# A hybrid encoder step: the forget-gate chain in five parts, a square sum three pairs on, memory values moved, and half of w_xo split there

## The chip, the cores and the metric

The kernel runs on one core of a Trainium2 chip. The metric is the device time of one execution in microseconds (us). Engines are named PE (TensorE, matmul), ACT (ScalarE), DVE (VectorE), POOL (GpSimd) and SP (SyncE, which issues most of the loads).

## The reference: what is computed

One layer on 512 prompt frames and 32 sample frames (544 columns in all), width 2048, in f32:

```python
gb, gc, hin, q, k, v = splits of rmsnorm(x) @ w_in           # 6 x 1024 outputs, 8 more for the gate
logf = log_sigmoid(z[..., o6:] + b_f)                        # 8 heads x 544 frames
yc = gb * short_conv(gc * hin)                               # 3 taps
ya = fox_attention(q, k_all, v_all, cumsum(logf))            # softmax with a forget bias
x += concat(rmsnorm(yc, g_conv_out), rmsnorm(ya, g_attn_out)) @ w_out
mk, mv = splits of rmsnorm(mem) @ w_xkv                      # 256 memory tokens, 4 heads
x += softmax(q_x mk) mv @ w_xo
x += square(relu(rmsnorm(x) @ w_up)) @ w_down
y = rmsnorm(x, g_final)
```

`logf`, the keys and values, the last conv rows and the memory keys and values are outputs too.

## The kernel before

Columns are the 544 frames, handled as two halves of 272. Each f32 product is made from three matmuls: operands are split into a high part (`hi`, fp32r, an ACT copy) and a low part (`lo`, a DVE subtraction), and hi·hi, hi·lo and lo·hi are summed in PSUM. `split` (L84, L85) makes both; for weights the tiles are called `whi` and `wlo`, four buffers each, one per 512 columns. A weight tile is loaded by SP into one of three `raw` buffers (128x1024, 512 KB), `weights` (L93) and `raw_block` (L220).

Where two output blocks share inputs, `seven` (L240) replaces eight block products by seven (Strassen's scheme): seven products of 24 matmuls each, called here X(b11), Y(t1), X(t2), Y(b22), X(t3), Z(b21), X(t4). The weights of t2 and b22 are sums `s2` and `s4` that DVE makes (L230); X and Y are copied out between products by ACT as `p15` and `u23` (`p` and `u` in the profile; L259, L263), so the next product into X or Y waits for that copy. The 22 pairs of the input projection (0 to 21, about 21 us each, from about 72 us) and the MLP's up projection run so. The trace order of each engine is what the scheduler of the tile framework made of the program's order; each engine works its instructions strictly in that order.

The gate: `emit_logf` makes the 8 extra outputs before the pairs; `chain_logf` (L357), called behind pair 0, turns them into `logf` and its running sums: z, e, Exp, w, Ln, a correction with a RECIPROCAL, two scans (`cum`, `cs`), the negated `neg` and `ncs` for later DMAs. `turn_logf`, behind pair 1, transposes `cum`. The readers are the attention heads, after pair 21.

The conv group: `on_gb` squares each gated block into `acc_c`; behind pair 9, the last conv pair, `rb_c = rstd(acc_c)` makes 1/rms by a square-sum matmul (`ssq`, L176), Ln and Exp on ACT and four DVE operations per half. Its reader is the output projection after pair 21.

Cross-attention (from 823 us): memory keys (L785, `w_xk`), memory values (L799, `w_xv`, eight raw tiles of 12 matmuls of 512 columns), four queries `xq` (`w_xq`, eight raw tiles), and per head scores, softmax, transposes and values, placed between the queries by hand. Then `w_xo`: 16 output blocks of 24 matmuls, eight raw tiles, two blocks each. Behind each block `xo_done` adds it to x (`x2r`, L938), squares it into `acc_3` and, for every second block, makes the operands of the MLP's `seven` (`operands`, L199). `rb_3 = rstd(acc_3)` comes behind the last block and before the first `seven` unit of the MLP.

Of the kernel before, what the change touches and what calls it, by code (L numbers as in the profile page):

```python
# [41 lines left out]
def hybrid_step(  # L42
# [156 lines left out]
    def operands(x, b11, ts, tags):  # L199
        hi, lo = two(b11)[:, 0], two(b11)[:, 1]  # L200
        split(hi, lo, x[:, 0])
        t = ts.rearrange("p (a b c) -> p a b c", a=2, b=2)
        x4 = x.rearrange("p (a b) c -> p a b c", a=2)
        dve.tensor_tensor(t[:, :, 0], x4[:, :, 1], x4[:, 0], ALU.subtract)
        for a in range(2):
            dve.tensor_tensor(t[:, a, 1], x[:, 3 - a], t[:, 0, a], ALU.subtract)
        o = {"b11": (hi, lo)}
        o["b21"], o["b22"] = both(x[:, 2:], tags[1])
        o["t1"], o["t2"] = both(t[:, 0], tags[0])
        o["t3"], o["t4"] = both(t[:, 1], tags[2])  # L210
        return o
# [6 lines left out]
    def raw_block(src, pl, tag):  # L218
        raw = pl.tile([128, 1024], F32, tag=tag, name=tag, bufs=3 if tag == "raw" else 4)
        sp.dma_start(raw, src)  # L220
        return raw
# [18 lines left out]
    def seven(pl, ops, ws, out, scale, mid, prefetch):  # L240
# [25 lines left out]
        product(X, w, "t2", False)  # L266
        act.activation(u23[:, 0], X, AF.Copy)
# [89 lines left out]
    def chain_logf(z16):  # L357
        z, lf, e, w = tmp("z"), tmp("lf"), tmp("e"), tmp("w")
        z, lf, e, w = z[:8, :T], lf[:8, :T], e[:8, :T], w[:8, :T]
# [114 lines left out]
    for i, pair in enumerate(pairs):  # L474
# [315 lines left out]
    ps = mm_tile()  # L790
    for p in range(8):
        hi, lo = weights(w_xv[p])
        for kk in range(2):
            k = 2 * p + kk
            c = slice(512 * kk, 512 * kk + 512)
            for t in range(2):
                d = slice(128 * t, 128 * t + 128)
                for n, (x, w) in enumerate(((mem[k][0], hi), (mem[k][0], lo), (mem[k][1], hi))):
                    pe.matmul(ps[:, t], x[:, d], w[:, c], start=k == 0 and n == 0, stop=k == KD - 1 and n == 2)  # L799
    for t in range(2):  # L800
        mf = tmp("mv")[:, :512]
        dve.tensor_scalar(mf, ps[:, t], rcol[:, t:t + 1], None, ALU.mult)
        pool.dma_start(o_mv[128 * t:128 * t + 128], mf)
        split(mvs[t][0], mvs[t][1], mf)
# [28 lines left out]
    def x_scores(h, q):  # L833
        P = xp.tile([128, 4, NMEM], F32, tag="P", name="xP")
# [19 lines left out]
    def x_transpose(h, P):  # L854
        PT = []
        for kt in range(2):
# [3 lines left out]
            hi = xp.tile([128, SEQ], F32R, tag=f"pth{kt}", name="xpth")  # L860
            lo = xp.tile([128, SEQ], F32R, tag=f"ptl{kt}", name="xptl")
# [4 lines left out]
    def x_values(h, PT):  # L866
# [35 lines left out]
    for h in range(HX):  # L902
        qs[h] = evac_xq(h, xq(h))
        if h == HX - 1:
            Pss = xs_scores()
            sa(h)
            sb(h - 1)
            sc(h - 1)
        else:
            sa(h)  # L910
            if h < HX - 2:
                sb(h)
                sc(h)
# [22 lines left out]
    def xo_done(m, ps):  # L936
# [5 lines left out]
        if i == 0:  # L942
            xgs[j] = up.tile([128, 4, TH], F32, tag="form", name="x")
# [43 lines left out]
    def plain(m, h):  # L987
        f = up.tile([128, 2, 2, TH], F32R, tag="form", name="form")
# [5 lines left out]
    def forms(i, h1, h2):  # L994
# [9 lines left out]
        for x, (j, k) in ((t12, (1, 2)), (b, (5, 3)), (t34, (4, 6))):  # L1004
            f = up.tile([128, 2, 2, TH], F32R, tag="form", name="form")
# [25 lines left out]
    up_cm.__exit__(None, None, None)  # L1031

# [241 lines left out]
```

## Time and profile before

| | us |
|---|---|
| three runs | 2391.26, 2392.85, 2392.91 |
| median | 2392.85 |
| profiled execution | 2392.07 |
| its span | 2390.3 |
| PE busy in the span | 2325.7 |
| DVE busy | 2017.8 |
| ACT busy | 1303.1 |

The span is the time from the first to the last instruction that the profiler saw; 1.8 us of the profiled execution lie around it. All other times are counted from its start. PE's granted clock is 2.4 GHz at 1.00 and 1.2 GHz at 0.50.

### The profile page before, as it was taken

How to read it: one execution, taken by the hardware profiler on the slowest of the kernel's cores; microseconds unless marked ns; L12 is line 12 of the kernel's file. 1: busy time of each engine (PE TensorE's matmuls, PEld its weight loads, DVE VectorE, ACT ScalarE, POOL GpSimd, SP SyncE). 2: the span in 40 equal slices, each digit the busy share in tenths (PEclk: the TensorE clock that was granted, in tenths of full speed). 3: DMA queues.
4: the chain of work that ended last, by engine and by line, in shares of the span. 5: the costliest groups of instructions: out<-in, count | busy, mean ns of one | idle time of the engine just before them, and what ended most of it. 6: DMA issues, size and time to landing. Idle time of an engine off the chain costs nothing.

```text
span 2390.3 us, 47513 instructions
## 1 busy us (share of the span) xinstructions
PE 2325.7 (97%) x18147; PEld 2295.4 (96%) x18147; DVE 2017.8 (84%) x3561; ACT 1303.1 (55%) x2524; POOL 197.0 (8%) x382
## 2 busy tenths in 40 slices
PE   8799999999999999899999999999999999999997
PEld 8699989999999998799999999999999999999997
DVE  9888988886767665989999999998598898888887
ACT  8345445554555444756666665666255555555555
POOL 0000011112300000001111111111000000000000
PEclk9899999999999999899999999999999999999999
DMA  5323345548715453446565556565956546646524
GB/s 176 106 99 125 110 133 157 162 153 317 235 62 166 139 168 127 158 142 203 190 203 186 184 194 204 191 201 172 351 191 237 174 152 237 214 131 219 177 84 137
DMA packets 160484, 416.34 MB, mean 174 GB/s; under 512 B 19384, under 2 KB 24368, under 8 KB 160256
## 3 DMA queue, kind: packets, MB, share of 16 engines
q1 hardware_dynamic: 110752, 313.87, 39.2%
q0 software_dynamic: 44000, 90.52, 12.0%
q10 hardware_dynamic: 5504, 8.93, 1.0%
q8 instruction: 142, 2.33, 0.4%
q14 instruction: 86, 0.70, 0.1%
HBM read 319.91 MB, written 93.33 MB: 173 GB/s over the span
## 4 chain that ended last, share of the span: by engine, by line
PE 91%; DVE 5%; DMA 1%; ACT 1%; issue 1%; DVEq 0%; SPq 0%; ACTq 0%
PE mmx L247 26%; PE dx L1083 14%; PE mmy L247 13%; PE mm L120 13%; PE mm L1083 11%; PE mmz L247 7%; PE mm L1177 2%; PE mm L785 1%; PE mm L799 1%; DVE wlo L85 1%; DVE opl L85 1%; PE s L532 1%; PE mm L311 1%; PE h L311 1%; PE o L588 1%
## 5 line engine op out<-in xcount | busy, mean ns | idle before, releaser
L84 ACT ACTIVATE whi<-raw 128x512 fp32r<-128x512 f32 x668 | 420.6, 632 | 498.8 <-PE mmx L247 97.1
L84 ACT ACTIVATE whi<-sum 128x512 fp32r<-128x512 f32 x656 | 409.9, 630 | 432.4 <-PE mmx L247 205.3
L85 DVE TENSOR_TENSOR wlo<-raw,whi 128x512 fp32r<-128x512 f32 x668 | 457.0, 688 | 137.6 <-ACT whi L84 125.6
L85 DVE TENSOR_TENSOR wlo<-sum,whi 128x512 fp32r<-128x512 f32 x656 | 439.6, 685 | 77.8 <-ACT whi L84 74.9
L247 PE MATMUL mmx<-oph,whi 128*128 128x272 f32 x1296 | 375.3, 290 | 20.1 <-ACT p L259 20.1
L247 PE MATMUL mmx<-oph,wlo 128*128 128x272 f32 x1296 | 375.9, 290 | 2.3 <-DVE wlo L85 2.3
L247 PE MATMUL mmx<-opl,whi 128*128 128x272 f32 x1296 | 373.8, 288 | 0.0
L1083 PE MATMUL dx<-f,whi 128*128 128x272 f32 x1792 | 344.4, 288 | 0.0
L1083 PEld LDWEIGHTS dx<-f,whi 128*128 128x128 f32 x1792 | 281.6, 188 | 0.0
L247 PEld LDWEIGHTS mmx<-oph,whi 128*128 128x128 f32 x1296 | 246.1, 190 | 21.2 <-ACT p L259 21.2
L1083 PE MATMUL mm<-f,whi 128*128 128x272 f32 x1344 | 259.6, 288 | 0.0
L1083 PE MATMUL dx<-f,wlo 128*128 128x272 f32 x896 | 258.5, 289 | 0.0
L247 PE MATMUL mmy<-oph,whi 128*128 128x272 f32 x864 | 250.9, 290 | 1.4 <-ACT whi L84 1.4
L247 PE MATMUL mmy<-oph,wlo 128*128 128x272 f32 x864 | 250.0, 289 | 0.7 <-DVE wlo L85 0.7
L247 PE MATMUL mmy<-opl,whi 128*128 128x272 f32 x864 | 249.4, 289 | 0.0
L247 PEld LDWEIGHTS mmx<-oph,wlo 128*128 128x128 f32 x1296 | 245.4, 189 | 2.7 <-DVE wlo L85 2.7
L247 PEld LDWEIGHTS mmx<-opl,whi 128*128 128x128 f32 x1296 | 245.5, 189 | 0.0
L1083 PEld LDWEIGHTS mm<-f,whi 128*128 128x128 f32 x1344 | 210.8, 188 | 0.0
L1083 PE MATMUL mm<-f,wlo 128*128 128x272 f32 x672 | 193.4, 288 | 0.0
L1083 PEld LDWEIGHTS dx<-f,wlo 128*128 128x128 f32 x896 | 168.9, 189 | 0.0
L247 PEld LDWEIGHTS mmy<-oph,whi 128*128 128x128 f32 x864 | 164.0, 190 | 2.0 <-ACT whi L84 1.8
L247 PE MATMUL mmx<-b,whi 128*128 128x272 f32 x864 | 165.0, 288 | 0.0
(381 smaller groups left out, 5175.2 us busy)
## 6 DMA issues: line engine op xcount, KB each, us to landing
raw<-in_w_up SPq DMA_DIRECT2D x128, 512.0 KB, 3.9
raw<-in_w_dn SPq DMA_DIRECT2D x112, 512.0 KB, 4.3
f<-fd SPq DMA_DIRECT2D x196, 272.0 KB, 5.7
fd<-form POOLq DMA_DIRECT2D x168, 272.0 KB, 4.0
raw<-in_w_in SPq DMA_DIRECT2D x88, 512.0 KB, 3.8
raw<-in_w_out SPq DMA_DIRECT2D x32, 512.0 KB, 4.3
raw<-in_w_ends SPq DMA_DIRECT2D x20, 512.0 KB, 4.1
kq<-hl POOLq DMA_DIRECT2D x32, 256.0 KB, 3.0
```

The costliest lines, as they stand in the source:

```text
L84: act.activation(hi, src, AF.Copy)
L85: dve.tensor_tensor(lo, src, hi.bitcast(F32), ALU.subtract)
L120: pe.matmul(ps[a], w, two(x)[:, a], start=first and n == 0, stop=last and n == 2)
L247: pe.matmul(ps, a[:, c], x, start=first and j == 0 and n == 0, stop=j == 7 and n == 2, skip_group_check=not first)
L311: pe.matmul(ps[a], w[:, c], xs[a][q], start=j + i == 0 and n == 0, stop=j + i == 8 and n == 2)
L532: pe.matmul(s[:, :N], q[a][:, c], k[b][:, :N], start=n == 0, stop=n == 2)
L588: pe.matmul(o[:, 128 * kt:], a[:, c], b, start=kt == 0 and n == 0, stop=False)
L785: pe.matmul(ps[:, 0, :NMEM], w[:, c], x, start=k == 0 and n == 0, stop=k == KD - 1 and n == 2)
L799: pe.matmul(ps[:, t], x[:, d], w[:, c], start=k == 0 and n == 0, stop=k == KD - 1 and n == 2)
L1083: pe.matmul(ps, a[:, c], f[:, x], start=first and j == 0 and n == 0, stop=j == 3 and n == 2, skip_group_check=not first)
L1177: pe.matmul(ps, w[:, c], two(x)[:, a], start=k == 0 and j == 0, stop=k == 3 and j == 2)
```

## The change

Five things. (1) `chain_logf` becomes `gate_open`, `gate_exp`, `gate_log`, nothing and `gate_close`, called behind pairs 0, 1, 2, 3 and 4. The tiles z, e, w move to other pools, and `neg` is made by DVE instead of ACT. (2) `rb_c` is made three pairs later. (3) `mem_values` becomes a function, called after the four queries and the scores, and head by head the transposes, values and first w_xo blocks follow it. (4) Inside it four of the eight w_xo tiles are loaded and split into `woh` and `wol` in slots of operands that are free by then (`presplit`). (5) `rstd(acc_3)` moves into the first MLP unit, behind its product t2 (`between`); some tiles change pool (`ring`), and `operands` makes t1, t2 before b21, b22.

```diff
-    def seven(pl, ops, ws, out, scale, mid, prefetch):
+    def seven(pl, ops, ws, out, scale, mid, prefetch, between=None):
...
         product(X, w, "t2", False)
+        if between:
+            between()
         act.activation(u23[:, 0], X, AF.Copy)
...
+    def gate_open(z16):
+        z = gate["z"] = npool.tile([128, T], F32, tag="rstd", name="z", bufs=3)[:8]
+        e = gate["e"] = new_acc()[:8]
...
         dve.scalar_tensor_tensor(e, z, -1.0, z, ALU.mult, ALU.min)
+
+    def gate_exp():
...
         act.activation(e, e, AF.Exp)
         dve.tensor_scalar(w, e, 1.0, None, ALU.add)
...
+    def gate_log():
...
         act.activation(lf, w, AF.Ln)
         dve.scalar_tensor_tensor(e, w, -1.0, e, ALU.add, ALU.subtract)
         dve.reciprocal(w, w)
...
-        act.activation(neg, cum[:8, :SEQ], AF.Copy, scale=-1.0)
-        pool.dma_start(ncd, neg)
...
+        dve.tensor_scalar(neg[:, :SEQ], cum[:, :SEQ], -1.0, None, ALU.mult)
+        pool.dma_start(ncd, neg[:, :SEQ])
...
+    def gate_close():
...
-        act.activation(hl[0], cs[:8, :LS], AF.Copy, scale=-1.0)
+        act.activation(hl[0], cs[:, :LS], AF.Copy, scale=-1.0)
...
-        return cum
+        turn_logf(gate["cum"])
...
-        if i == 0:
-            cum = chain_logf(z16)
-        if i == 1:
-            turn_logf(cum)
+        if i < 5:
+            (lambda: gate_open(z16), gate_exp, gate_log, lambda: None, gate_close)[i]()
         if n2 == "gb" and j2 == 7:
             pool.dma_start(o_conv, newc)
+        if i == len(pairs) - 9:
             rb_c = rstd(acc_c, DC)
...
+    def mem_values():
+        ps = mm_tile()
+        for p in range(8):
+            hi, lo = weights(w_xv[p])
...
+            if 2 <= p < 6:
+                wos.append(presplit(w_xo[p - 2]))
...
+    def presplit(src):
+        raw = raw_block(src, None, "raw")
+        his, los = [], []
+        for c in range(0, 1024, 512):
+            hi, lo = slot("B", F32R, "woh")[:, :512], slot("C", F32R, "wol")[:, :512]
+            split(hi, lo, raw[:, c:c + 512])
...
+        sa(h)
+    Pss = xs_scores()
+    mem_values()
...
-            wo = weights(w_xo[i // 2])
+            wo = wos[i // 2] if i < 8 else weights(w_xo[i // 2])
...
-    rb_3 = rstd(acc_3, D)
+    rb_3 = []
...
     for i in range(4 * CH):
         h1, h2 = tmp("h1")[:, :T], tmp("h2")[:, :T]
         nxt = seven(up, ops, nxt, (h1, h2), (relu, relu), lambda h: act.activation(h, h, AF.Square),
-                    lambda: fetch_up(i + 1))
+                    lambda: fetch_up(i + 1), (lambda: rb_3.append(rstd(acc_3, D))) if i == 0 else None)
```

The order of the instructions on the engines changes with it at three places.

ACT in pair 1, before: `ych`, `sq` belong to the conv block, `e`, `lf`, `neg`, `ncs` to the gate, `p15` is the copy of X (L259) that the next X product waits for.

```order
L87 ACTIVATE ych_1386<-h2_1117,vec_78 128x544
L187 ACTIVATE sq_1392<-h2_1117 128x544
L84 ACTIVATE whi_1543<-sum_1481 128x512
L84 ACTIVATE whi_1547<-sum_1481 128x512
L365 ACTIVATE e_1397<-e_1397 8x544
L367 ACTIVATE lf_1396<-w_1398 8x544
L375 DMA lfs_1416<-in_clogf 8x256
L380 ACTIVATE neg_1420<-cum_1415 8x512
L386 ACTIVATE ncs_1425<-cs_1423 8x288
L259 ACTIVATE p15_1436<-mmx_1433 128x272
```

After, the same stretch (L373 is the gate's Exp, in a tile named `acc`):

```order
L87 ACTIVATE ych_1386<-h2_1117,vec_78 128x544
L187 ACTIVATE sq_1392<-h2_1117 128x544
L259 ACTIVATE p15_1409<-mmx_1406 128x272
L84 ACTIVATE whi_1516<-sum_1454 128x512
L84 ACTIVATE whi_1520<-sum_1454 128x512
L263 ACTIVATE p15_1409<-mmy_1407 128x272
L373 ACTIVATE acc_1396<-acc_1396 8x544
L84 ACTIVATE whi_1549<-sum_1489 128x512
L84 ACTIVATE whi_1553<-sum_1489 128x512
```

The `p15` copy of X stands right behind `sq`, that of Y two weights later, and of the gate only the Exp is left here, behind both.

DVE in pair 3, before, from the conv block's square (`acc_993`) on; `wlo_2057` and `wlo_2061` are the low halves of the weights of the second X product, t2.

```order
L163 TENSOR_TENSOR acc_993<-acc_993,sq_1931 128x544
L85 TENSOR_TENSOR wlo_2026<-sum_1952,whi_2025 128x512
L85 TENSOR_TENSOR wlo_2057<-sum_1994,whi_2056 128x512
L230 TENSOR_TENSOR sum_2064<-raw_1944,raw2_1946 128x1024
L85 TENSOR_TENSOR wlo_2061<-sum_1994,whi_2060 128x512
L230 TENSOR_TENSOR sum_2220<-raw2_2214,raw2_2216 128x1024
L85 TENSOR_TENSOR wlo_2092<-sum_2029,whi_2091 128x512
L85 TENSOR_TENSOR wlo_2096<-sum_2029,whi_2095 128x512
```

After; here `wlo_2036` and `wlo_2040` are that product's low halves, `w_1672`, `acc_1396`, `lf_1945` and `z_1395` are tiles of the gate.

```order
L163 TENSOR_TENSOR acc_993<-acc_993,sq_1897 128x544
L85 TENSOR_TENSOR wlo_2005<-sum_1918,whi_2004 128x512
L383 RECIPROCAL w_1672<-w_1672 8x544
L230 TENSOR_TENSOR sum_2043<-raw_1910,raw2_1912 128x1024
L384 TENSOR_TENSOR acc_1396<-acc_1396,w_1672 8x544
L85 TENSOR_TENSOR wlo_2036<-sum_1973,whi_2035 128x512
L385 TENSOR_TENSOR lf_1945<-lf_1945,acc_1396 8x544
L85 TENSOR_TENSOR wlo_2040<-sum_1973,whi_2039 128x512
L386 SCALAR_TENSOR_TENSOR lf_1945<-z_1395,lf_1945 8x544
L85 TENSOR_TENSOR wlo_2071<-sum_2008,whi_2070 128x512
L389 COPY lfs_1675<-lf_1945 8x32
L393 SCALAR_TENSOR_TENSOR z_1395<-ones_86,lf_1945 8x512
```

The RECIPROCAL, a sum and a multiplication of the gate now stand between the square and the low half for t2, the scans behind that of the product after it.

ACT in the memory values, before: `whi` of one w_xv tile follows that of the last.

```order
L84 ACTIVATE whi_10971<-raw_10969 128x512
L84 ACTIVATE whi_10975<-raw_10969 128x512
L84 ACTIVATE whi_10993<-raw_10991 128x512
L84 ACTIVATE whi_10997<-raw_10991 128x512
L84 ACTIVATE whi_11015<-raw_11013 128x512
L84 ACTIVATE whi_11019<-raw_11013 128x512
L84 ACTIVATE whi_11037<-raw_11035 128x512
L84 ACTIVATE whi_11041<-raw_11035 128x512
```

After, `woh` is the high half of a w_xo tile; `raw_11663` and `raw_11695` are w_xv tiles, `raw_11685` and `raw_11717` w_xo tiles.

```order
L84 ACTIVATE whi_11665<-raw_11663 128x512
L84 ACTIVATE woh_11687<-raw_11685 128x512
L84 ACTIVATE whi_11669<-raw_11663 128x512
L84 ACTIVATE woh_11691<-raw_11685 128x512
L84 ACTIVATE whi_11697<-raw_11695 128x512
L84 ACTIVATE whi_11701<-raw_11695 128x512
L84 ACTIVATE woh_11719<-raw_11717 128x512
L84 ACTIVATE woh_11723<-raw_11717 128x512
```

The first `woh` of a w_xo tile stands between the two halves of a w_xv tile.

## Rows read from the trace of the kernel before

**Rows 1.** The profile page: the span, its first line of busy time (engine, busy us, share of the span, instructions), and the share of the engines in the chain that ended last.

```profile
span 2390.3 us, 47513 instructions
...
PE 2325.7 (97%) x18147; PEld 2295.4 (96%) x18147; DVE 2017.8 (84%) x3561; ACT 1303.1 (55%) x2524; POOL 197.0 (8%) x382
...
PE 91%; DVE 5%; DMA 1%; ACT 1%; issue 1%; DVEq 0%; SPq 0%; ACTq 0%
```

**Rows 2.** Who waited for whom, TensorE alone, over the whole span: engine, line, what was waited for; us in total, times, longest us.

```profile
PE mmx L247 <- ACT p L259: 20.1, 5, 15.3
...
PE ssq L176 <- DVE acc L163: 6.9, 2, 5.3
```

**Rows 3.** Timeline of TensorE around pair 1: start us, duration us, instruction; the last bracket is the idle time before it and what ended it.

```profile
96.63 0.29 PE L247 MATMUL mmy<-oph,whi 128*128 128x272 f32 x1
...
99.53 0.29 PE L247 MATMUL mmy<-oph,wlo 128*128 128x272 f32 x1
115.10 0.59 PE L247 MATMUL mmx<-oph,whi 128*128 128x272 f32 x1 [15.29 <-ACT p L259]
...
120.24 0.29 PE L247 MATMUL mmy<-oph,whi 128*128 128x272 f32 x1
```

**Rows 4.** Timeline of ScalarE in pair 1, same columns.

```profile
101.76 0.66 ACT L365 ACTIVATE e<-e 8x544 f32<-8x544 f32 x1 [1.40 <-DVE e L364]
...
113.68 0.63 ACT L380 ACTIVATE neg<-cum 8x512 f32<-8x512 f32 x1 [9.71 <-DVE cum L378]
...
114.68 0.37 ACT L259 ACTIVATE p<-mmx 128x272 f32<-128x272 f32 x1
```

**Rows 5.** Timeline of VectorE in pair 1, same columns (x2: two instructions in one row).

```profile
96.53 1.29 DVE L85 TENSOR_TENSOR wlo<-sum,whi 128x512 fp32r<-128x512 f32 x2
97.74 0.48 DVE L363 TENSOR_SCALAR z<-pz,vec 8x272 f32<-8x272 f32 x1
...
99.89 1.20 DVE L230 TENSOR_TENSOR sum<-raw,raw 128x1024 f32<-128x1024 f32 x1
...
105.59 3.53 DVE L369 RECIPROCAL w<-w 8x544 f32<-8x544 f32 x1
...
112.44 1.21 DVE L378 TENSOR_TENSOR_SCAN cum<-ones,lf 8x512 f32<-8x512 f32 x1
113.58 0.72 DVE L383 TENSOR_TENSOR_SCAN cs<-ones,lfs 8x288 f32<-8x288 f32 x1
```

**Rows 6.** Timeline of TensorE around pair 1's `pz` matmuls and at pair 10, same columns.

```profile
92.49 1.08 PE L362 MATMUL pz<-z,sel 16*8 16x272 f32 x4
...
307.53 0.29 PE L247 MATMUL mmx<-b,wlo 128*128 128x272 f32 x1
313.16 2.18 PE L176 MATMUL ssq<-acc,inv 128*128 128x272 f32 x4 [5.35 <-DVE acc L163]
...
319.27 0.29 PE L247 MATMUL mmx<-oph,whi 128*128 128x272 f32 x1
```

**Rows 7.** Stretches: from:to, length, busy us of PE (instructions), PEld, DVE, ACT and POOL, granted clock, DMA share, GB/s. The first is a stretch inside pairs 3 and 4, the second the end of cross-attention, the third its output projection, the fourth the first MLP unit.

```profile
150.00:170.00 20.00, 20.00 (x162) 20.00 (x161) 17.53 (x29) 10.50 (x20) 1.09 (x2) 1.00 0.40 133
928.00:946.40 18.40, 15.87 (x115) 12.51 (x114) 10.33 (x26) 7.82 (x23) 0.00 (x0) 1.00 0.21 70
945.00:998.00 53.00, 48.30 (x351) 47.07 (x350) 50.40 (x89) 41.17 (x71) 0.00 (x0) 0.94 0.71 242
998.00:1024.00 26.00, 19.68 (x112) 18.29 (x111) 23.13 (x39) 12.94 (x25) 0.00 (x0) 0.80 0.17 63
```

**Rows 8.** Timeline of VectorE in pair 3, same columns as above.

```profile
155.32 0.72 DVE L163 TENSOR_TENSOR acc<-acc,sq 128x544 f32<-128x544 f32 x1
...
160.15 1.29 DVE L85 TENSOR_TENSOR wlo<-sum,whi 128x512 fp32r<-128x512 f32 x2
```

**Rows 9.** The timeline rows of TensorE that end an idle time in pair 4 and in the output projection; and three stretches with the columns of rows 7.

```profile
182.53 0.40 PE L247 MATMUL mmx<-oph,whi 128*128 128x272 f32 x1 [1.41 <-ACT p L259]
...
969.65 0.57 PE L120 MATMUL mm<-oh,whi 128*128 128x272 f32 x1 [2.15 <-DVE x2r L938]
...
180.80:186.80 6.00, 4.59 (x37) 4.38 (x36) 5.97 (x10) 3.94 (x8) 1.06 (x2) 1.00 0.81 270
969.60:973.00 3.40, 3.35 (x15) 3.38 (x16) 3.40 (x7) 2.14 (x4) 0.00 (x0) 0.50 0.54 164
...
1013.90:1020.80 6.90, 5.82 (x25) 5.82 (x26) 4.66 (x7) 1.23 (x3) 0.00 (x0) 0.51 0.43 152
```

**Rows 10.** Timeline of ScalarE in the memory values (three rows), and the landing of their weights: name, queue, count, KB each, median us from issue to landing.

```profile
858.37 1.16 ACT L84 ACTIVATE whi<-raw 128x512 fp32r<-128x512 f32 x2 [2.10 <-DMA raw<-in_w_xv]
...
863.96 0.63 ACT L84 ACTIVATE whi<-raw 128x512 fp32r<-128x512 f32 x1 [0.76 <-DVE wlo L85]
...
866.74 0.63 ACT L84 ACTIVATE whi<-raw 128x512 fp32r<-128x512 f32 x1 [0.76 <-DVE wlo L85]
...
raw<-in_w_xv SPq DMA_DIRECT2D x8, 512.0 KB, 4.4
```

**Rows 11.** VectorE between the first x2r add and the first MLP unit: three timeline rows (x2, x4: so many instructions in one row).

```profile
946.43 0.72 DVE L938 TENSOR_TENSOR x2r<-x2r,mm 128x544 f32<-128x544 f32 x1 [1.44 <-PE mm L120]
...
1010.59 0.78 DVE L179 TENSOR_TENSOR nt<-rstd 128x272 f32<-128x272 f32 x2
...
1014.25 2.49 DVE L85 TENSOR_TENSOR wlo<-sum,whi 128x512 fp32r<-128x512 f32 x4
```

More of the change, by code (lines that the diff above doesn't have):

```diff
@@ L218, in raw_block @@
     def raw_block(src, pl, tag):
-        raw = pl.tile([128, 1024], F32, tag=tag, name=tag, bufs=3 if tag == "raw" else 4)
+        raw = (pl or wpool).tile([128, 1024], F32, tag=tag, name=tag, bufs=3 if tag == "raw" else 4)
         sp.dma_start(raw, src)
@@ L364, in chain_logf @@
         dve.scalar_tensor_tensor(e, z, -1.0, z, ALU.mult, ALU.min)
+    def gate_exp():
+        e = gate["e"]
+        w = gate["w"] = pj.tile([128, T], F32, tag="hl", name="w", bufs=4)[:8]
         act.activation(e, e, AF.Exp)
         dve.tensor_scalar(w, e, 1.0, None, ALU.add)
+        gate["lfs"] = tmp("lfs")
+        act.dma_start(gate["lfs"][:8, :PAST], clogf)
+    def gate_log():
+        z, e, w = gate["z"], gate["e"], gate["w"]
+        lf = tmp("lf")[:8, :T]
         act.activation(lf, w, AF.Ln)
@@ L768, in hybrid_step, with ring, flat @@
     mpool_cm.__exit__(None, None, None)
+    ring_cm = tc.tile_pool(name="ring", bufs=3, side="right")
+    ringp = ring_cm.__enter__()
     xpool_cm = tc.tile_pool(name="cross", bufs=1, side="right")
     xp = xpool_cm.__enter__()
+    def ring(name, dt=F32R):
+        return ringp.tile([128, 2, 2, TH], dt, tag="form", name=name)
+    def flat(x):
+        return x.rearrange("p a b -> p (a b)")
     rb_2 = rstd(acc_2, D)
@@ L789, in hybrid_step @@
         split(xh_[0][:, h], xh_[1][:, h], mf)
[L790 to L804, printed above, removed]
+    def mem_values():
+        ps = mm_tile()
+        for p in range(8):
+            hi, lo = weights(w_xv[p])
+            for kk in range(2):
+                k = 2 * p + kk
+                c = slice(512 * kk, 512 * kk + 512)
+                for t in range(2):
+                    d = slice(128 * t, 128 * t + 128)
+                    for n, (x, w) in enumerate(((mem[k][0], hi), (mem[k][0], lo), (mem[k][1], hi))):
+                        pe.matmul(ps[:, t], x[:, d], w[:, c], start=k == 0 and n == 0, stop=k == KD - 1 and n == 2)
+            if 2 <= p < 6:
+                wos.append(presplit(w_xo[p - 2]))
+        for t in range(2):
+            mf = tmp("mv")[:, :512]
+            dve.tensor_scalar(mf, ps[:, t], rcol[:, t:t + 1], None, ALU.mult)
+            pool.dma_start(o_mv[128 * t:128 * t + 128], mf)
+            split(mvs[t][0], mvs[t][1], mf)
+    wos = []
+    def presplit(src):
[4 more added lines that the diff above has]
+            split(hi, lo, raw[:, c:c + 512])
+            his.append(hi)
+            los.append(lo)
+        return Parts(his), Parts(los)
     x2g = []
@@ L903, in hybrid_step @@
         qs[h] = evac_xq(h, xq(h))
[L904 to L908, printed above, removed]
-        else:
[L910 to L913, printed above, removed]
+        sa(h)
+    Pss = xs_scores()
+    mem_values()
+    for h in range(HX):
+        if h < 3:
+            o = ring("o")
+            ox.append((flat(o[:, 0]), flat(o[:, 1])))
+        else:
+            ox.append([npool.tile([128, T], F32R, tag="rstd", name="o", bufs=3) for n in range(2)])
     x3d = [dpool.tile([128, T], F32, name=f"x3d{m}", tag=f"x3d{m}") for m in range(KD)]
@@ L942, in xo_done @@
         if i == 0:
-            xgs[j] = up.tile([128, 4, TH], F32, tag="form", name="x")
+            xgs[j] = up.tile([128, 2 * T], F32, tag="sum", name="x").rearrange("p (a b) -> p a b", a=4)
         act.activation(xgs[j][:, 2 * i:2 * i + 2], two(x), AF.Identity, scale=gain(G_MLP, m))
@@ L947, in xo_done @@
             ops.append(operands(xgs.pop(j), b11, up.tile([128, 2 * T], F32, tag="sum", name="ts"), "ABC"))
-    ox.append((slot("A", F32R, "oh"), slot("A", F32R, "ol")))
+    order = [m for j in range(8) for m in (j, j + 8)]
+    sb(0)
     PTs = samp_transpose(xp, Pss, NMEM)
+    sb(1)
+    sc(0)
     osx = samp_values(xp, PTs, cmvt, None)
+    sb(2)
+    sc(1)
     ot = samp_out(osx)
@@ L954, in hybrid_step @@
         split(ox[i][0][:, SEQ:], ox[i][1][:, SEQ:], ot[:, 32 * i:32 * i + 32])
-    order = [m for j in range(8) for m in (j, j + 8)]
-    wo = None
+    sb(3)
+    sc(2)
     early = []
     for i in range(2):
-        if i % 2 == 0:
-            wo = weights(w_xo[0])
         ps = mm_tile()
         c = slice(512 * i, 512 * i + 512)
-        early.append((ps, (wo[0][:, c], wo[1][:, c])))
+        early.append((ps, (wos[0][0][:, c], wos[0][1][:, c])))
         xo_part(ps, early[i][1], 0, 3)
         if i == 0:
-            sb(3)
             sc(3)
@@ L987, in plain @@
     def plain(m, h):
[L988 removed]
+        f = ring("form")
         hi, lo = (f[:, n].rearrange("p a b -> p (a b)") for n in range(2))
```

42 lines of the change are left out of this document (19 added, 23 removed).

## The prediction

> **What bounds the kernel now.** I read the page's totals first. TensorE (PE) is busy for 97% of the span and holds 91% of the chain that ended last [rows 1], so only time in which PE stands still, or runs at its lower clock, can be won. The second view is the list of PE's waits: the longest entry, X waiting for ScalarE's (ACT) copy `p`, has one wait of 15.3 us in its 20.1 us, and the square-sum matmul has one of 5.3 us in 6.9 [rows 2]. The third view is the timelines around the long waits.
>
> The long wait lies in pair 1. PE ends its Y product at 99.53 and starts the next X product only at 115.10 [rows 3]. That product then runs at 1.2 GHz: its 24 matmuls take until 120.24, 5.1 us, where Y before it took 3.0 us. From the start of Y to the start of the product after X is 23.6 us instead of 6.0, so 17.6 us are lost. ACT shows why [rows 4]: its copies `p` (L259, L263) stand behind `neg` (L380), which sat idle 9.71 us for VectorE's (DVE) scan. DVE spends 3.53 us on a RECIPROCAL of 8x544 and 1.21 and 0.72 us on the two scans [rows 5]. PE does not need that chain at all; it needs the `p` copies queued behind it.
>
> A second loss lies at pair 10, where `rb_c` is made: PE ends X at 307.53, waits 5.35 us with the square-sum matmul at the head of its queue for DVE's `acc`, and runs at 1.2 GHz afterwards, so that X(s2) starts at 319.27 [rows 6].
>
> The third lies in the output projection of cross-attention and the first MLP unit. DVE is busy 50.40 of 53 us there and 23.13 of the 26 us behind, while PE's clock is granted at 0.94 and 0.80 [rows 7]. DVE bounds this stretch, not PE.
>
> **Part 1, gate chain.** The 17.6 us go: no `p` waits for the chain any more, since `neg` is on DVE, Ln in pair 3 and `ncs` in pair 5. What is late next is the low half of the weights. In pair 1 the order puts wlo of s2 behind z, z, ych, acc, e and a sum. From the rows [rows 5] I count 97.13 (the wlo before has ended its first 0.60 start-to-start) + 2 z (0.8) + ych 0.8 and acc 0.65 (128x544), e 0.65, sum 1.15 + wlo 0.65 = 101.8. PE wants it for the third matmul of X, at 99.9. That is 1.9 us lost (bounds 0 and 3.6, the latter if the clock drops as well, see below).
>
> In pair 3 the order puts the RECIPROCAL, a sum and a multiply ahead of wlo of s2. There DVE ended acc at 156.04 and PE needed that wlo at 160.15, where its rows began in the old order [rows 8]: 156.0 + wlo 0.6 + 3.46 + 1.15 + 0.65 + 0.65 = 162.5, so 2.3 us late. Then two more 8x544 operations, the two scans (1.15 and 0.65 start to start) and `neg` make the second half of the next product's wlo about 1 us late. An idle of 2.15 us at 969.65 was followed by a stretch at clock 0.50, one of 1.41 us at 182.53 by one at 1.00 [rows 9]; so I expect one slow stretch behind the 2.3 us, 1.7 us lost in its 3.4 us, partly covering the late wlo. I take 3.7 us, with bounds 0 and 10 (all of the chain's DVE time on the path). The other operations (z, Exp, Ln, ncs) cost nothing: DVE and ACT idle beside PE there. The memory traffic is the same. Part 1: -17.6 + 1.9 + 3.7 = -12.0 us, from -17.6 to -6.
>
> **Part 2, `rb_c` three pairs later.** In pair 10 the wait of 5.35 us, the square-sum's four matmuls and the slow Y go. Y then starts right behind X at 307.66, takes 3.0, and X(s2) waits for `p` about 1.57 us as in pair 4 (1.41 idle [rows 9] and the start behind it), which gives 312.2 instead of 319.27: -7.0 us. In pair 14 the four matmuls stand inside a product and cost what the four `pz` do, 1.0 us [rows 6]; `acc` has been final since pair 10, so nothing is waited for. The reader of `rb_c`, the output projection, begins only behind pair 21. Part 2: -6.0 us, bounds -6.1 and -1 (if the wait comes back at its new place).
>
> **Part 3, memory values moved, half of w_xo split there.** PE's work is the same, so the stretch before the first x2r add (946.43, rows 11) keeps its length unless waits change. It held 2.5 us of PE idle at its end [rows 7], from a chain of short dependent steps per head; most of it goes, since the four heads' transposes, values and w_xo matmuls are now interleaved. New waits come with the memory values: PE eats one raw tile of w_xv in 2.78 us (two halves of 1.39 [rows 10]), and now four w_xo tiles pass through the same three raw buffers. A buffer's turn is landing 4.4 us, plus two halves of about 0.6, plus the last wlo 0.7: 6.3 us, so twelve tiles through three buffers take 25.2 us, and PE has 22.2 us of values and 2.2 of scores. That is near balance, and ACT works in order: it stands at a woh whose tile hasn't landed while the second half of the next w_xv tile waits. Following the order tile by tile I get three waits of about 1.2, 1.2 and 2.2 us, less 0.9 of transposes that run beside the last, plus 0.9 for the split of the values behind them: 4.6 us (bounds 0 and 9). Against the 2.5 idle and some 2.5 lost between short groups before, the first x2r add comes at about 946, 0.4 earlier (bounds: 3.4 earlier, 6 later).
>
> A sentence on the page's price for a landing. The trace lands 512 KB in 4.4 us [rows 10]. The Trainium skill (DMA: Bandwidth & Descriptors, "Anatomy of one DMA — SWDGE (gpsimd) path") fits a DMA as about 2.0 us plus bytes over 436 GB/s, 3.2 us for 512 KB; by it (an estimate from that page) each raw wait would be 1.2 us shorter and the total some 3 us lower. These loads go by another queue than the page's fit, and the measured 4.4 decides.
>
> Behind the first add, DVE is the bound until the first MLP unit's second weights at 1014.25: 67.8 us from 946.43 [rows 11]. Eight of its wlo leave the stretch (start to start 0.60: 4.8 us) and the eight rstd operations from 1010.59 to 1013.11 (2.5 us) are pushed behind t2, where DVE has slack in the second half of the unit. ACT loses its eight woh too. Part 3: -0.4 - 4.8 - 2.5 = -7.7 us; bounds -14 (the clock also stays up: two slow stretches of 1.7, and 3 more at the first add) and +5 (DVE's share is worth 1 and the first add is 6 late).
>
> **Sum.** -12.0 - 6.0 - 7.7 = -25.7. The profiled execution took 2392.07 us (span 2390.3 and 1.8 around it), 0.8 below the median of the three runs, 2392.85. So 2366.4 from the profiled run, and 2367.1 from the median; I say 2366.5.
>
> **Rivals.**
> (a) No new waits: DVE is ahead when it comes to the RECIPROCAL, and the operands of part 3 gain a little more. For it: DVE was busy 17.53 of 20 us around pair 3 [rows 7]; against it, its order is fixed and the RECIPROCAL stands ahead of the wlo. -17.6 - 6.1 - 10 gives 2359.
> (b) The gate's DVE work lands wholly on the path in pair 3 (10 instead of 3.7) and pair 1 drops the clock (3.6 instead of 1.9): 2366.5 + 8 gives 2374.5. For it: PE takes a new wlo every 1.5 us there (half a product of 3.0), and the RECIPROCAL alone is 3.53.
> (c) The output projection doesn't speed up: memory values come late, or PE's slow clock, not DVE, sets the pace. Part 3 at 0 gives 2374, at +5 gives 2379. For it: PE's clock fell to 0.50 there [rows 9]; against it, DVE's 50.40 of 53.
> (d) The square sum only moves its wait: 2371.5. Against it: `acc` is final three pairs earlier.
> (e) Slower than before: raw buffers starve PE through the memory values. With a tile's turn at 6.3 us the three buffers balance PE; if the turns don't overlap, because ACT stands at a woh whose tile was issued only after a release, the twelve tiles go one by one, 12 x 6.3 = 75.6 us against PE's 24.4: 51.2 us of waits in place of 4.6, total 2413. It decides against the change from the point where the waits reach 4.6 + 25.7 = 30.3 us, that is a turn of (24.4 + 30.3) / 12 x 3 = 13.7 us, twice mine. For it: one wait of 2.10 us for a w_xv tile already stands in the trace with eight tiles [rows 10]. Against it: the issues are independent.
>
> **How the numbers follow.** The forecast has 0.60, (a) 0.10, (b) 0.08, (c) 0.12, (d) 0.04, (e) 0.06. Range 2354 to 2383: the lower end is the three parts at their best bounds (-17.6 - 6.1 - 14), the upper end (c) with a part of (b); it leaves out most of (e) and about a tenth besides. Within 0.2% (4.8 us, about what a measurement of this kernel tells from no change) means 2388 to 2397.6: only a milder (e) or (b) and (c) together reach there. Faster 0.93 (all but that), same 0.03, slower 0.04.
>
> **What would show it.** In the profile after: the 15.3 us entry of X waiting for `p` is gone, and in its place are two entries of X waiting for wlo of about 2 us each, in pairs 1 and 3, the latter with a stretch at clock 0.5; no wait of the square sum over 1 us, and X(s2) of pair 10 some 7 us earlier relative to its X; memory values with three waits of 1 to 2 us for whi or woh and at most 30 us long; from the first x2r add to the first unit's s2 weights about 60 us instead of 67.8. I am wrong if the pair 3 entry is above 6 us, if memory values take over 32 us, or if that last distance stays above 65.

## The result, and where the time went

The changed kernel took 2367.11 us (median of four runs, 2365.94 to 2370.54), the kernel before 2392.88 beside it. The ratio is 0.9895, 95% interval 0.9878 to 0.9912. The forecast was 2366.5, with a range of 2354 to 2383. The profiled execution of the changed kernel took 2366.74, its span 2365.0.

The page after, the same lines as in [rows 1]:

```profile
span 2365.0 us, 47489 instructions
PE 2317.7 (98%) x18147; PEld 2287.3 (97%) x18147; DVE 2015.4 (85%) x3562; ACT 1300.5 (55%) x2523; POOL 196.9 (8%) x382
...
PE 91%; DVE 5%; DMA 2%; ACT 1%; issue 1%; SPq 0%; DVEq 0%; ACTq 0%
```

PE runs the same 18147 matmuls, and DVE and ACT are as busy as before: no work was taken away. Of the 25.3 us by which the span fell, 17.3 are PE's idle time. The other 8.0 are its busy time: the same matmuls ran for less time at the lower clock (mean granted clock 0.996 instead of 0.988). Who waited for whom, TensorE alone, over the whole span after (us in total, times, longest), to be held against [rows 2]:

```profile
...
PE mmx L247 <- ACT p L259: 6.0, 4, 2.1
PE mmx L247 <- DVE wlo L85: 3.9, 5, 1.6
...
PE mmy L247 <- ACT whi L84: 2.8, 2, 2.1
PE mm L120 <- DVE x2r L973: 2.6, 2, 2.3
PE ssq L176 <- DVE acc L163: 1.5, 1, 1.5
...
PE xo L911 <- ACT mv L84: 1.0, 1, 1.0
PE mm L825 <- ACT whi L84: 0.7, 2, 0.6
```

X's 15.3 us for `p` and the square sum's 5.3 us for `acc` are gone. The square sum's 1.5 us that is left was the other of its two waits before. The memory values (L825) waited 0.7 us for their weights in all.

A table by stage says more than the totals. A pair is counted from the start of its X(b11) to that of the next; the starts are read from PE's timeline of either kernel.

| stage | before | after | change | forecast |
|---|---|---|---|---|
| start of pair 0 | 69.41 | 70.03 | +0.6 | 0 |
| pair 1 | 39.19 | 22.99 | -16.2 | -15.7 |
| pair 3 | 21.06 | 24.01 | +2.95 | +3.7 |
| pair 4 | 22.74 | 23.82 | +1.1 | 0 |
| pair 10 | 29.66 | 22.74 | -6.9 | -7.0 |
| pair 14 | 21.06 | 21.96 | +0.9 | +1.0 |
| pair 21 to the first matmul on the memory | 278.71 | 279.37 | +0.7 | 0 |
| from there to the first x2r add | 122.84 | 122.12 | -0.7 | -0.4 |
| first x2r add to the end of the first MLP unit | 85.82 | 77.70 | -8.1 | -7.3 |
| behind it, to the start of PE's last matmul | 1345.05 | 1344.55 | -0.5 | 0 |

Pairs 0, 2 and 5 changed by 0.1 or less, the others not at all. The sum is -26.2 us at the last matmul; 0.9 of it is given back between that and the end of the span. The changes of 0.7 and 0.5 us in the two long stages are within what the runs below show there with edits that touch neither (278.3 to 280.8 and 1344.5 to 1345.7 us).

In pair 3 the new wait looks like this on PE (start, duration, instruction, idle before it and what ended it):

```profile
145.31 0.39 PE L247 MATMUL mmy<-oph,whi 128*128 128x272 f32 x1 [0.63 <-ACT p L263]
...
146.82 0.39 PE L247 MATMUL mmx<-oph,wlo 128*128 128x272 f32 x1 [1.00 <-DVE wlo L85]
...
152.08 0.40 PE L247 MATMUL mmy<-oph,wlo 128*128 128x272 f32 x1 [0.50 <-DVE wlo L85]
```

and on DVE so:

```profile
140.92 3.53 DVE L383 RECIPROCAL w<-w 8x544 f32<-8x544 f32 x1
144.39 1.15 DVE L230 TENSOR_TENSOR sum<-raw,raw 128x1024 f32<-128x1024 f32 x1
145.46 0.70 DVE L384 TENSOR_TENSOR acc<-acc,w 8x544 f32<-8x544 f32 x1
146.09 0.67 DVE L85 TENSOR_TENSOR wlo<-sum,whi 128x512 fp32r<-128x512 f32 x1
```

PE's matmul at 146.82 starts when the wlo of 146.09 is done; ahead of that wlo stand the three rows that the order shows. Four stretches of the profile after (columns as in [rows 7]). The first lies in pair 3 and ran at the full clock; the second is the memory values, the third the output projection, the fourth the first MLP unit:

```profile
140.00:160.00 20.00, 17.87 (x139) 17.21 (x138) 19.97 (x28) 9.14 (x17) 1.55 (x3) 1.00 0.37 116
883.50:911.60 28.10, 27.00 (x126) 20.55 (x125) 20.03 (x38) 16.26 (x36) 0.00 (x0) 1.00 0.63 193
928.80:977.10 48.30, 45.48 (x343) 44.41 (x342) 45.88 (x81) 36.17 (x63) 0.00 (x0) 0.96 0.65 215
977.10:1006.50 29.40, 24.64 (x175) 23.53 (x174) 28.93 (x49) 17.15 (x33) 0.00 (x0) 0.94 0.27 91
```

DVE is busy 19.97 of 20 us in pair 3 and 28.93 of 29.4 in the first unit: it bounds both.

### The profile page after: what moved, and what is told of

The parts are those of the page before. It is cut to its first block, busy times and chain, and to the rows that moved or that the text cites. A ratio compares the mean times of both kernels' runs of the same rounds, so it can differ in the third digit from the quotient of the medians.

```text
span 2365.0 us, 47489 instructions
## 1 busy us (share of the span) xinstructions
PE 2317.7 (98%) x18147; PEld 2287.3 (97%) x18147; DVE 2015.4 (85%) x3562; ACT 1300.5 (55%) x2523; POOL 196.9 (8%) x382
## 4 chain that ended last, share of the span: by engine, by line
PE 91%; DVE 5%; DMA 2%; ACT 1%; issue 1%; SPq 0%; DVEq 0%; ACTq 0%
PE mmx L247 26%; PE dx L1121 14%; PE mmy L247 13%; PE mm L120 12%; PE mm L1121 11%; PE mmz L247 7%; PE mm L1215 2%; PE mm L313 1%; PE h L313 1%; PE mm L810 1%; PE s L548 1%; DVE wlo L85 1%; PE o L604 1%; DVE opl L85 0%; DMA kq<-kq 0%
## 5 line engine op out<-in xcount | busy, mean ns | idle before, releaser
L84 ACT ACTIVATE whi<-raw 128x512 fp32r<-128x512 f32 x660 | 415.3, 632 | 489.3 <-PE mmx L247 96.9
L85 DVE TENSOR_TENSOR wlo<-raw,whi 128x512 fp32r<-128x512 f32 x660 | 451.7, 688 | 125.2 <-ACT whi L84 117.3
```

The source lines that it names most:

```text
L84: act.activation(hi, src, AF.Copy)
L85: dve.tensor_tensor(lo, src, hi.bitcast(F32), ALU.subtract)
```

## The experiments

Each kernel is the changed one with the edit shown; the kernel before ran beside them on the same chip (medians 2392.02 to 2392.82). The table by pair separates effects that the total time would not: the changed kernel's runs reached from 2365.94 to 2370.54 us in one group of four and from 2367.44 to 2368.16 in another.

**Old gate chain.** Undo part 1 alone. The chain is one function again, called as before; of the edit only the calls are shown.

```diff
-        if i < 5:
-            (lambda: gate_open(z16), gate_exp, gate_log, lambda: None, gate_close)[i]()
+        if i == 0:
+            cum = chain_logf(z16)
+        if i == 1:
+            turn_logf(cum)
```

> The changed kernel with the old gate chain (one function behind pair 0, its negation on ACT, the transposes behind pair 1); all else as changed. Theory (the chain cost 15.8 us in pair 1, and its five parts cost 2.9 us in pair 3 and 0.65 in pair 4): 12.2 us slower than the changed kernel, about 2379.3, one wait of X for p of about 15 us back, the waits for wlo in pair 3 gone. Rival (the new waits in pairs 3 and 4 are not the gate's, they come from the other edits): they stay, and the kernel is 15.8 us slower, about 2382.9.

Measured: 2379.39 us, ratio to before 0.9948 (0.9933 to 0.9962), 12.3 slower than the changed kernel. Pair 1 is back at 38.7 us, pair 3 at 21.06, pair 4 at 22.74. PE's timeline:

```profile
116.33 0.60 PE L247 MATMUL mmx<-oph,whi 128*128 128x272 f32 x1 [15.29 <-ACT p L259]
```

So the 15.3 us are the chain's, and the new waits in pairs 3 and 4 are too. The theory held, the rival fell.

**`rb_c` behind pair 9 again.** Undo part 2 alone. With 22 pairs `len(pairs) - 9` is 13, so the change makes `rb_c` behind pair 13: four pairs later, not three.

```diff
-        if i == len(pairs) - 9:
+        if n2 == "gb" and j2 == 7:
             rb_c = rstd(acc_c, DC)
```

> The changed kernel with rb_c made behind pair 9 again. Theory (7.0 us lost in pair 10, 0.95 saved in pair 14): 6.1 us slower, about 2373.2, the wait of the square sum for acc near 5 us and a stretch at clock 0.5 behind it. Rival (the wait came from the old gate's shift of the work): less than 2 us slower, under 2369.

Measured: 2375.75 us (0.9932, 0.9918 to 0.9947), 8.6 slower. Pair 10 is 29.9 us long, pair 14 is 21.06: +7.2 and -0.9, so 6.3 where the theory has 6.1. The first MLP unit, which the edit does not touch, took 1.3 us longer in this profile than in the changed kernel's: a stretch of 3.4 us at clock 0.50 lay at 999.7 us, behind the low half of s2, where the changed kernel had none. The rest is within the runs' spread. PE's timeline at pair 10 repeats [rows 6] to the hundredth:

```profile
301.80 2.18 PE L176 MATMUL ssq<-acc,inv 128*128 128x272 f32 x4 [5.35 <-DVE acc L163]
```

**No early split.** Undo part 4 of the change; the memory values stay where they are now.

```diff
-            if 2 <= p < 6:
-                wos.append(presplit(w_xo[p - 2]))
...
-            wo = wos[i // 2] if i < 8 else weights(w_xo[i // 2])
+            wo = weights(w_xo[i // 2])
```

> The changed kernel without the early split: all eight w_xo tiles are loaded and split where they are used, memory values stay in their new place. Theory (DVE bounds the output projection): eight wlo of 0.60 come back, 4.8 us longer from the first x2r add to the first unit's s2 weights, and the first add some 1 us earlier since four tiles fewer pass during the memory values: about 2371. Rival 1 (the place of the memory values gives the gain, DVE's share does not): within 1 us of 2367. Rival 2 (raw buffers starve the memory values): faster than the changed kernel, about 2365.

Measured: 2369.67 us (0.9908, 0.9893 to 0.9922), 2.6 slower; the four runs, 2367.80 to 2371.63, overlap the changed kernel's, so the signs rest on the stages. From the first x2r add to the end of the first unit it takes 81.87 us instead of 77.70: +4.2 where 4.8 were reckoned. The first add comes 120.58 us behind the first matmul on the memory instead of 122.12: the four tiles cost 1.5 us while they pass beside the memory values. Both signs are as the theory has them; together they make 2.6.

**`rstd(acc_3)` before the first unit again.**

```diff
-    rb_3 = []
+    rb_3 = [rstd(acc_3, D)]
...
-                    lambda: fetch_up(i + 1), (lambda: rb_3.append(rstd(acc_3, D))) if i == 0 else None)
+                    lambda: fetch_up(i + 1))
```

> The changed kernel with rstd(acc_3) before the first MLP unit again. Theory (its eight DVE operations stand ahead of the sums and wlo of t2): 2.5 us slower, and up to 1.7 more if the longer idle lowers the clock, 2369.5 to 2371.3. Rival (DVE has slack there, ACT's copies or the operands set the pace): within 0.7 us of 2367.1.

Measured: 2372.37 us (0.9919, 0.9903 to 0.9936), 5.3 slower. The loss is all in the first unit: 33.89 us instead of 29.34, and 33.82 in the kernel before. The low half of s2 comes at 993.36, 64.2 us behind the first add, against 991.15 and 62.3 in the changed kernel: 1.8 us. The other 2.7 lie behind it, where the clock differs: PE idles 1.66 us ahead of its first matmul with that low half, and the stretch there is granted at 0.50:

```profile
994.10 0.59 PE L247 MATMUL mmx<-oph,wlo 128*128 128x272 f32 x1 [1.66 <-DVE wlo L85]
```

```profile
993.10:999.90 6.80, 5.80 (x25) 5.80 (x26) 4.58 (x7) 1.27 (x3) 0.00 (x0) 0.50 0.45 157
```

**Reciprocal on ACT.** This tells which of the gate's operations made the wait in pair 3.

```diff
-        dve.reciprocal(w, w)
+        act.activation(w, lf, AF.Exp, scale=-1.0)
         dve.tensor_tensor(e, e, w, ALU.mult)
```

> The changed kernel with the gate's RECIPROCAL on DVE (3.53 us) replaced by exp(-ln w) on ACT. Theory (the RECIPROCAL makes the late wlo of pair 3): pair 3 falls from 24.0 to 21.1 us, about 2.9 us faster, near 2364.2, pair 4 keeps its 23.8. Rival (the scans and the other operations of the chain take the time): pair 3 stays above 23 us.

Measured: 2363.08 us (0.9880, 0.9863 to 0.9896), 4.0 faster than the changed kernel. Pair 3 is 21.06 us, as without any gate; pair 4 fell from 23.82 to 23.24 as well. DVE's timeline in pair 3, where the two wlo now stand in one row:

```profile
138.79 0.72 DVE L163 TENSOR_TENSOR acc<-acc,sq 128x544 f32<-128x544 f32 x1
139.43 1.46 DVE L85 TENSOR_TENSOR wlo<-sum,whi 128x512 fp32r<-128x512 f32 x2
140.80 0.70 DVE L384 TENSOR_TENSOR acc<-acc,w 8x544 f32<-8x544 f32 x1
```

The two scans and the rest of the chain still stand in that pair and cost PE nothing. So the wait needs the RECIPROCAL on DVE. The edit does not part it from the multiplication and the sum, 1.7 us that stood ahead of the wlo with it and stand behind it now.

**The conv block's split behind t2 of the next pair.** Pairs 4 and 7 lose 1.7 us in the kernel before too, by a wait of the same form as pair 1's, X for `p` [rows 9]; in the changed kernel pairs 7 and 10 lose 1.7 by it and pair 4 loses 2.8.

```diff
-        kinds[n2][1](j2, h2)
+        if n2 == "gb":
+            later.append(lambda j=j2, h=h2: on_gb(j, h))
+        else:
+            kinds[n2][1](j2, h2)
```

(`later` is handed to the next `seven` as its `between`.)

> The changed kernel with the split and square of each gated conv block, where it comes second in its pair, called behind product t2 of the next pair instead of ahead of it. Theory (ACT stands at that block's split, which waits for DVE, while the p copies that X needs are queued behind it, the same form of wait as the old gate chain's): pairs 4, 7 and 10 fall from 23.8, 22.7 and 22.7 to 21.1 us and pair 1 from 23.0 to about 21.5, some 7 us faster, near 2360. Rival (the wait only moves to u or to wlo): less than 2 us faster.

Measured: 2361.38 us (0.9869, 0.9854 to 0.9884), 5.7 faster than the changed kernel. Pairs 1, 7 and 10 are 21.2, 21.06 and 21.06 us, pair 4 21.67; pair 3 rose by 0.7 to 24.7. PE's waits from 90 to 330 us, first of the changed kernel, then of this one:

```profile
PE mmx L247 <- ACT p L259: 4.9, 3, 2.1
PE mmx L247 <- DVE wlo L85: 1.6, 2, 1.0
PE mmy L247 <- ACT p L263: 1.3, 2, 0.7
PE mmy L247 <- DVE wlo L85: 0.5, 1, 0.5
```

```profile
PE mmx L247 <- DVE wlo L85: 1.0, 1, 1.0
PE mmy L247 <- ACT p L263: 0.6, 1, 0.6
```

No wait of X for `p` is left; of what was won in pairs 1, 4, 7 and 10 only the 0.7 us in pair 3 came back. There PE idled less than in the changed kernel, but a slow stretch followed:

```profile
143.58 0.40 PE L247 MATMUL mmy<-oph,whi 128*128 128x272 f32 x1 [0.63 <-ACT p L263]
145.09 0.57 PE L247 MATMUL mmx<-oph,wlo 128*128 128x272 f32 x1 [0.99 <-DVE wlo L85]
```

```profile
145.10:148.60 3.50, 3.50 (x15) 3.50 (x16) 3.50 (x6) 0.63 (x1) 0.52 (x1) 0.51 0.84 287
```

The profile shows something else that the edit did not aim at: the output projection had no slow stretch here.

```profile
923.49:970.60 47.11, 44.33 (x342) 43.03 (x341) 45.58 (x81) 35.96 (x63) 0.00 (x0) 1.00 0.66 219
```

It was 1.2 us shorter than the changed kernel's 48.4, but the low half of s2 came 62.3 us behind the first add all the same, and the first MLP unit took 1.2 us longer. So the slow stretch in the projection costs nothing: DVE sets the pace up to that low half.

**Operands in the old order.**

```diff
-        o["t1"], o["t2"] = both(t[:, 0], tags[0])
         o["b21"], o["b22"] = both(x[:, 2:], tags[1])
+        o["t1"], o["t2"] = both(t[:, 0], tags[0])
```

(The subtraction that makes the last part of `t` goes back ahead of them too.)

> The changed kernel with the operands in the old order (b21, b22 ahead of t1, t2). Theory (the order of the last block's operands is the same DVE work, and the second product waits for sums and wlo): within 1 us of 2367.1. Rival (t1 and t2 first bring part of the first unit's 4.5 us): first MLP unit above 31 us instead of 29.3, 2 us slower or more.

Measured: 2364.75 us (0.9885, 0.9870 to 0.9899), 2.4 faster. Neither: the new order costs something. The first unit takes 27.97 us instead of 29.34. The low half of s2 starts 61.0 us behind the first add (988.96 after 928.00) instead of 62.3, which is the whole of the 1.4 us: from there to its end the unit takes 15.4 us in both kernels. DVE does the first rstd operation behind those wlo and not ahead of the sums. Why the old order brings it forward was not followed.

**Memory values ahead of the queries again, without the early split.**

```diff
+    mem_values()
     wos = []
...
     Pss = xs_scores()
-    mem_values()
```

> The changed kernel without the early split, as u_presplit, and with the memory values back ahead of the queries; to be read against u_presplit (2369.67). Theory (the new place is worth little by itself, it makes room for the early split; the transposes beside its end are worth about 1 us): from the first memory matmul to the first x2r add 121.5 to 123 us instead of 120.6, 1 to 2 us slower than u_presplit. Rival (the place gives most of part 3): 4 us slower or more.

Measured: 2372.91 us (0.9915, 0.9901 to 0.9930), 3.2 slower than the kernel without early split. From the first matmul on the memory to the first x2r add it takes 125.69 us instead of 120.58, 5.1 more; the first unit gave back 1.3, as the low half of s2 comes 65.3 us behind the first add here and 66.5 there. I had reckoned 1 to 2; the rival's 4 is nearer. PE's waits from 905 to 931 us, where the last head's scores, the transposes and the values now follow each other with nothing between:

```profile
PE pts L640 <- DVE xsP L923: 2.7, 1, 2.7
PE xs L881 <- ACT xqh L84: 1.5, 1, 1.5
PE xpt L898 <- ACT xP L886: 0.2, 1, 0.2
```

Here the clock fell as well:

```profile
913.00:919.90 6.90, 6.11 (x33) 4.71 (x34) 3.11 (x7) 1.79 (x3) 0.00 (x0) 0.51 0.01 2
```

So the memory values are cover: 22 us of matmuls that wait for none of it, between the softmax and its first reader.

**All three improvements at once.** Reciprocal on ACT, the conv block's split deferred, operands in the old order, by the diffs above.

> The changed kernel with three edits at once: the gate's reciprocal as exp(-ln w) on ACT, the conv block's split and square behind t2 of the next pair, and the operands in the old order. If the three gains lie in different stages (2.9 in pair 3; 1.8, 2.2, 1.7 and 1.7 in pairs 1, 4, 7 and 10; about 1.4 in the first MLP unit) they add up: some 11.5 us faster than the changed kernel, near 2355.5, with all pairs from 1 on at 21.1 but 14. If they share a wait, less than 8 us: above 2359.

Measured: 2354.93 us, ratio to before 0.9844 (0.9830 to 0.9859), 12.7 faster than the changed kernel beside it; singly the three gave 4.0, 5.7 and 2.4, so they add up. PE's list of waits between 90 and 330 us is empty. Pairs 1 and 3 are 21.16 and 21.06, pairs 7 and 10 21.06, pair 4 21.49. First x2r add to the end of the first unit: 76.02 us against 77.82 in the run beside it.

**The changed kernel again,** unaltered, as the measure of the runs' spread.

> The changed kernel itself, unaltered, on the same chip as the run beside it: 2367.1 within 1.5 us, and its stages as in its first profile, pair by pair within 0.1 us; the first MLP unit, whose slow stretch need not fall the same way, within 1.5.

Measured: 2367.66 us (0.9898, 0.9881 to 0.9914). All pairs from 1 on agree with the first profile to 0.02 us, the first unit took 29.55 instead of 29.34.

## Why the prediction was right, step by step

**Pair 1** (-15.7 forecast, -16.2 measured). Shown by undoing part 1: the 15.3 us came of the chain's copies that stood ahead of `p` on ACT. That `neg` was the one that mattered is read from [rows 4] and was not tried alone. Before, the pair was 18.1 us longer than an undisturbed one of 21.06; 17.6 were counted. What takes the wait's place is the low half of s2, as forecast, on PE and on DVE:

```profile
101.42 0.39 PE L247 MATMUL mmy<-oph,whi 128*128 128x272 f32 x1 [0.69 <-ACT p L263]
...
102.53 0.40 PE L247 MATMUL mmx<-oph,wlo 128*128 128x272 f32 x1 [0.59 <-DVE wlo L85]
```

```profile
101.80 2.48 DVE L85 TENSOR_TENSOR wlo<-sum,whi 128x512 fp32r<-128x512 f32 x4
```

PE runs two matmuls of Y(b22) ahead of the waiting one, so the list has entries of 0.69 and 0.59 us and not one of 2. The pair lost 1.9 us (22.99 against 21.06), as counted.

**Pair 3** (+3.7 forecast, +2.95 measured). The wait came where the order put it, and it goes with the RECIPROCAL. PE's third matmul of X(t2) was 2.3 us late (146.82 instead of 144.52, where it would have followed the two ahead of it), as counted. That PE needs this wlo at 160.15 in the kernel before is right, by PE's own row; the wlo that starts at 160.15 on DVE [rows 8] belongs to a later product.

```profile
160.15 0.29 PE L247 MATMUL mmx<-oph,wlo 128*128 128x272 f32 x1
```

What did not come is the lower clock, for which up to 1.7 us had been added: it stayed at 1.00. The idle time came in pieces of 0.63, 1.00 and 0.50 us, but that does not explain it: with the conv block's split deferred the first two pieces were the same and a slow stretch followed.

**Pair 4** (0 forecast, +1.1 measured). This was missing from the sum. I priced the chain's operations only where their own pair waits. All of it goes when the chain is undone, and half of it (0.6) with the RECIPROCAL, so that half is DVE work pushed on from pair 3; the other half was not followed.

**`rb_c`** (-7.0 and +1.0 forecast, -6.9 and +0.9 measured). Right in both, and shown by undoing it. The four matmuls in pair 14:

```profile
379.15 0.62 PE L176 MATMUL ssq<-acc,inv 128*128 128x272 f32 x2
...
380.36 0.62 PE L176 MATMUL ssq<-acc,inv 128*128 128x272 f32 x2
```

**To the first x2r add** (-0.4 forecast, -0.7 measured). The sum is near by luck; its terms were not.

```profile
823.59:946.43 122.84, 120.21 (x853) 110.53 (x852) 76.20 (x147) 59.71 (x126) 3.25 (x6) 1.00 0.40 129
```

```profile
806.72:928.84 122.12, 119.98 (x853) 110.20 (x852) 80.42 (x155) 63.22 (x133) 3.25 (x6) 1.00 0.46 146
```

The first row is the kernel before, the second the changed one. I had 4.6 us of waits in the memory values; there PE idled 1.1 us in 28.1 (27.00 busy), and 0.7 us of that was for weights. The w_xv tiles landed in 3.6 us instead of the 4.4 that I took from [rows 10], and eight transposes filled 1.4 us there where I had given them 0.9. On the other side I had 5.0 us of gains. The idle time at the end fell from 2.5 us to 1.0 and did not go almost wholly. The 2.5 us between short groups stand in no row: PE idled 2.6 us in the whole stretch before and 2.1 after, and its busy time fell by 0.2. Rival (e), raw buffers that starve PE, asked for tens of microseconds; the four tiles cost 1.5 us, by the experiment without the early split:

```profile
896.15 1.15 ACT L84 ACTIVATE whi<-raw 128x512 fp32r<-128x512 f32 x2 [2.21 <-DMA raw<-in_w_xv]
899.19 1.15 ACT L84 ACTIVATE woh<-raw 128x512 fp32r<-128x512 f32 x2 [1.88 <-DMA raw<-in_w_xo]
```

ACT does stand at tiles that have not landed, in turn, as feared, but early enough that PE loses only those 0.7 us by it.

The Trainium skill's fit for a DMA (DMA: Bandwidth & Descriptors, "Anatomy of one DMA — SWDGE (gpsimd) path"), 3.2 us for 512 KB by an estimate from it, lay below both landings, 3.6 and 4.2 us:

```profile
raw<-in_w_xv SPq DMA_DIRECT2D x8, 512.0 KB, 3.6
raw<-in_w_xo SPq DMA_DIRECT2D x8, 512.0 KB, 4.2
```

**From there to the end of the first MLP unit** (-7.3 forecast, -8.1 measured). The forecast was one distance, from the first add to the low half of s2, 67.8 us before and about 60 after. It was 62.3:

```profile
928.84 1.48 DVE L973 TENSOR_TENSOR x2r<-x2r,mm 128x544 f32<-128x544 f32 x2 [1.31 <-PE mm L120]
```

```profile
991.15 2.49 DVE L85 TENSOR_TENSOR wlo<-sum,whi 128x512 fp32r<-128x512 f32 x4
```

So 5.5 us of the 7.3 came there. Undone singly, the early split is worth 4.2 of my 4.8, the move of `rstd(acc_3)` 1.8 of 2.5, and the new order of the operands, which I did not see, costs 1.4. These make 4.6 of the 5.5, and the new place of the memory values, which lost 1.2 in its own experiment, leaves 3.4; the rest is open.

The other 2.6 us are the clock's, which I had only as a bound. From the low half of s2 to its end the unit takes 15.4 us in nine of the twelve profiles, at 1.00 there; it takes 18.0 in the kernel before and with `rstd(acc_3)` in its old place, where some 6.5 us of it are at 0.50. First the changed kernel, then that one:

```profile
991.15:1006.54 15.39, 15.05 (x119) 14.83 (x120) 15.30 (x29) 7.38 (x14) 0.00 (x0) 1.00 0.42 138
```

```profile
993.36:1011.37 18.01, 17.27 (x116) 17.27 (x117) 14.26 (x22) 7.02 (x13) 0.00 (x0) 0.82 0.35 118
```

In sum, 25.7 us were forecast and 25.3 measured between the two spans. The nearness owes something to misses that cancel: 0.75 too much in pair 3, 1.1 missing in pair 4, 0.5 too little in pair 1 and 0.8 at the end, and 1.7 us more in the stages that the forecast left at 0 and behind the last matmul. Of the rivals, (a) and (b) fell in pair 3, (c) fell with the early split, `rstd(acc_3)` and the full clock in the deferred kernel's projection, (d) fell in pair 14.

## What to carry to other kernels

Where an engine works in order, ask of every long wait what stands behind the waiting instruction, and not only what the wait is for: 15.3 us were lost because a copy of 0.4 us stood behind a chain that nobody needed for more than 400 us, and three waits of the same form, of 1.4 to 2.1 us, were still left to take. When a long chain is cut up, look for its one long operation: without the gate's RECIPROCAL of 3.53 us on DVE pair 3 had no wait, and moving that one to ACT gave 4.0 us. Independent matmuls, here the memory values, can cover the wait between a softmax and its first reader: in that place they made the stretch to the first x2r add 5.1 us shorter in this kernel. Where one engine hands over to another, measure up to the handover and behind it apart: DVE's work set the one part, PE's clock the other.

## What the runs showed of the hardware that I had not expected

A wait of X for `p` of 2.06 us in pair 4 left PE's clock at 1.00:

```profile
170.50 0.39 PE L247 MATMUL mmx<-oph,whi 128*128 128x272 f32 x1 [2.06 <-ACT p L259]
```

```profile
168.00:176.00 8.00, 5.94 (x48) 5.72 (x47) 7.96 (x13) 4.88 (x10) 1.61 (x3) 1.00 0.62 204
```

The 1.66 us of the kernel with `rstd(acc_3)` in its old place, shortly behind other idle times of 1.00 and 0.52 us, stood beside a stretch at 0.50. The idle times of 0.63 and 1.00 us in pair 3 left the clock at 1.00 in the changed kernel; 0.63 and 0.99 at the same place in the deferred one were followed by 0.50. So neither the longest idle time nor its pieces say by themselves whether the clock falls, and such a term is a bound and not a size.

A RECIPROCAL on 8 partitions took 3.53 us where the other DVE operations on the same 8x544 took 0.7. The pairs were otherwise steady: in two profiles of the changed kernel every pair from 1 on agreed to 0.02 us.
